# Scale and shift of a LayerNorm moved into the matmul that follows it, and factors formed from tiles already on the chip

## The chip, the cores and the metric

One program runs on one core of a Trainium2 chip. The core has five engines with their own in-order queues: TensorE (PE: matmuls, transposes; its weight loads, PEld, overlap them), VectorE (DVE), ScalarE (ACT), GpSimd (POOL) and SyncE (SP, which here only issues DMAs). They share an SBUF of 128 partitions; matmuls write to PSUM. The metric is the device time of one execution in microseconds (us), the median over the runs shown; lower is better.

## What is computed

One layer of a hybrid encoder on x of 512 tokens by 2048, in float32. Cut to what matters here:

```
h = rms_norm(x, g_mix)
q, k, v_sb, u, v_sg, gate_a, gate_b = split(h @ w_in)      # 1024 x5, 2048 x2 columns
o = stick_breaking_attention(rms(q) * g_q, rms(k) * g_k, v_sb)          # 8 heads
y_a = o @ w_oa
u, v = gelu(u), gelu(v_sg)
v = layer_norm(v, sgu_ln_g, sgu_ln_b)                      # over 1024 columns
w = where(mask, w_spatial, 0)                              # 8 groups of 128 x 128
mixed = einsum('gij,bcjgd->bcigd', w, chunks(v)) + b_spatial
y_b = (u * mixed) @ w_ob
x = x + (sigmoid(gate_a) * y_a + sigmoid(gate_b) * y_b) @ w_out
x = x + square(relu(rms_norm(x, g_ff) @ w_ff1)) @ w_ff2
```

The gain and the bias of the LayerNorm go by the column d of a group, the mixing sums over the token j. So gain[d] * (w @ v0) + bias[d] * (row sum of w) + b_spatial is the same number as w @ (v0 * gain + bias) + b_spatial, where v0 is v less its mean, times the reciprocal of its spread.

## The kernel before

**Split matmuls.** A float32 operand is held as two `float32r` tiles, hi and lo (`split_to`, L106: ACT casts hi at L108 or L111, DVE subtracts for lo at L109 or L112), and a product is three matmuls (`mm3`, L70: lines 72, 73, 74). Weights are loaded by SP, two 128-row pieces at a time (`weight`, L87: cast L94, subtraction L96).

**Stages.** `by_token` (L117) makes 512 columns of a projection for four blocks of 128 tokens in four PSUM accumulators (of five): eight weight loads, 24 matmuls each, then one evacuation per block. Its order is q, k, v of heads 0 to 3, then q, k, v of heads 4 to 7, then the two halves of `vg` (v_sg). Then come u and the gates, 256 columns at a time: the first pair with plain matmuls (`plain_pair`, L245), all others by a Strassen scheme (`strassen_columns`, L197) with seven products and three fork accumulators that `new_forks` opens (L288) in the second PSUM pool, `aux`, of three tiles. Then `ya`, `yb`, the output projection and the MLP.

**Work behind the matmuls.** `behind` is a queue of small steps; after each weight load's matmuls `step()` takes one, and `flush()` takes all that are left. Each engine gets its instructions about in the order in which they are written; a planner that knows dependences may let a ready one pass one that is not, but at run time every queue is in order.

- The attention of one half (`attention`, L521) is twelve such steps: `weights` (scores, sigmoids, a scan on DVE), `turn` (transposes, `aT` at L555) and `product` (L563), whose result `oT` POOL stores to DRAM (L569). That of half 0 runs beside the second q and k projections, that of half 1 beside `vg`.
- `save` (L481) adds hi and lo of the normalised input `hT` to a whole tile (L485) and stores it with POOL (L486) in `held_h`, four tiles to a step, in the first v projection.
- `gate_factors` (L596) fetches two of these whole tiles back with POOL (L478) and forms the four sums m7, m6, m4, m5 that the Strassen scheme needs for that pair (`factor`, L236: one DVE sum or difference at L242, then hi and lo). Eight such calls stand at steps 6, 8, 10, 11, 12, 13, 14 and 15 of the 16 steps of `vg`.
- `moved` (L587) copies some `hT` tiles out of the buffers for raw weights.

**The LayerNorm.** `evac_v` (L616) applies Gelu on ACT (L618) and leaves the eight tiles in SBUF. In the u stage `centred` (L633) takes their moments (`bn_stats` L636, `bn_aggr` L638) and normalises in place (L644); `normed` (L647) lets POOL multiply by the gain (L649), add the bias (L650), both held as broadcast rows, and store the tile (L651) in `held_v`. `spatial` (L665) transposes the mixing matrices (L668), masks them (L671 to L674) and splits them into `wsp`; it is a step of the u pair too.

**The mixing.** In the `ya` stage POOL fetches v and u again (`fetch_mix`), `split_mix` (L731) splits v, and `mixed` (L735) multiplies by the mixing matrices (L744, L746), adds the two PSUM halves and `bs`, the broadcast b_spatial, on DVE (L748, L750), and multiplies by u on POOL (L751). The evacuation of `ya` is a DVE product with the gate (L777).

**Buffers.** All tiles of 512 columns come from one pool, `slots`, of 64; twelve more are in `long`, where the first six `hT` pairs live. Raw weights have six buffers, of which three hold `hT` tiles 6 to 8 for a time.

Of the kernel before, what the change touches and what calls it, by code (L numbers as in the profile page):

```python
# [10 lines left out]
F32 = mybir.dt.float32  # L11
# [5 lines left out]
P = 128  # L17
# [5 lines left out]
SBW = 1024  # L23
# [12 lines left out]
def tile_hybrid_layer(ctx: ExitStack, tc: tile.TileContext, x, g_mix, w_in, g_q, g_k, ln_g, ln_b,  # L36
# [17 lines left out]
    def slot(name, dt=F32, pool=slots):  # L54
        return pool.tile([P, 512], dt, name=name, tag="slot")
# [10 lines left out]
    def f32(ap):  # L66
        return ap.bitcast(F32)
# [289 lines left out]


    gm = const.tile([16, P], F32, name="gm")
    gains = const.tile([32, P], F32, name="gains")  # L360
    gT = const.tile([P, 16], F32, name="gT")
    gT2 = const.tile([P, 32], F32, name="gT2")

    def turn_gains(src, dst):
        n = src.shape[0]
# [101 lines left out]
    win = w_in[0]  # L467


    held_h = dram.tile([KT, P, W], F32, name="held_h")  # L470
    held_o = dram.tile([HEADS, 2, P, W], F32, name="held_o")
    held_v = dram.tile([2, NTB, P, W], F32, name="held_v")
    held_g = dram.tile([(SGW + 2 * D) // P, P, W], F32, name="held_g")
# [4 lines left out]
        nc.gpsimd.dma_start(out=f32(t) if dt is F32R else t, in_=src)  # L478
        return t

    def save(k):  # L481
        t = slot("whole")
        for half, part in enumerate(hT[k]):
            hi, lo = (f32(x) for x in sides(part))
            nc.vector.tensor_tensor(out=t[:, half * HS:(half + 1) * HS], in0=hi, in1=lo, op=ALU.add)  # L485
        nc.gpsimd.dma_start(out=held_h[k], in_=t)  # L486

    def heads_of(c0, g0, half, name):

# [81 lines left out]
        steps = [[(weights, 0)], [], [(weights, 1)], [(turn, 0)], [(weights, 2)], [(product, 0), (turn, 1)], [(weights, 3)], [(product, 1), (turn, 2)], [], [(product, 2), (turn, 3)], [], [(product, 3)]]  # L571
        return [lambda fs=fs: [f(h) for f, h in fs] for fs in steps]

    for half in range(2):
        qT = heads_of(0, 16, half, "q")
        kT = heads_of(SBW, 24, half, "k")
        if half == 0:
            behind.extend([lambda k=k: [save(k + i) for i in range(4)] for k in range(0, KT, 4)])
        v = []
        by_token(win, 2 * SBW + half * W, hT_at, KT,  # L580
                 lambda tb, o, v=v: v.append(split(o, "v", rstd[:, tb:tb + 1])), "v")
        if half == 0:
            behind.extend(attention(half, qT, kT, v))

    hy = {}

    def moved(k):  # L587
        for half, part in enumerate(hT[k]):
            name = "y" + "12"[k % 2] + "12"[half]
            if LONG // 2 <= k < LONG // 2 + RAWH and name != "y12":  # L590
                t = slot("hT", F32R)
                nc.sync.dma_start(out=f32(t), in_=f32(part))
                part = t
            hy[name, k // 2] = part

    def gate_factors(k):  # L596
        whole = [fetched(held_h[2 * k + i], "whole") for i in range(2)]
        for name in ("m7", "m6", "m4", "m5"):
            factor(hy, whole, k, name, -1.0 if name in ("m7", "m4") else None)

    def at_steps(steps):
        behind.extend([lambda fs=steps.get(i, []): [f() for f in fs] for i in range(max(steps) + 1)])

    steps = collections.defaultdict(list)
    for i, f in enumerate(attention(half, qT, kT, v)):
        steps[i].append(f)
    for k in range(KT):
        steps[2 + k // 4].append(lambda k=k: moved(k))
    for k, i in enumerate((6, 8, 10, 11, 12, 13, 14, 15)):
        steps[i].append(lambda k=k: gate_factors(k))  # L610
    at_steps(steps)

    vg = {}
    VS = 3 * SBW + SGW
    for half in range(2):
        def evac_v(tb, o):  # L616
            t = slot("vg")
            nc.scalar.activation(out=t, in_=o, func=AF.Gelu, scale=rstd[:, tb:tb + 1])  # L618
            vg[tb, half] = t

        by_token(win, VS + half * W, hT_at, KT, evac_v, "vg")
    ref = state["load"]

    lng, lnb = [], []
    with tc.issue_after(ref.ins):
        for half in range(2):
            for src, dst, nm in ((ln_g, lng, "lng"), (ln_b, lnb, "lnb")):
                t = slot(nm)
                nc.sync.dma_start(out=t, in_=src[:, half * W:(half + 1) * W].to_broadcast([P, W]))
                dst.append(t)  # L630
    vn = {}

    def centred(tb):  # L633
        st = tiny(12, "st")
        for half in range(2):
            nc.vector.bn_stats(out=st[:, half * 6:half * 6 + 6], in_=vg[tb, half])  # L636
        mv = tiny(2, "mv")
        nc.vector.bn_aggr(out=mv, in_=st)  # L638
        ve = tiny(1, "ve")
        nc.vector.tensor_scalar(out=ve, in0=mv[:, 1:2], scalar1=EPS, scalar2=None, op0=ALU.add)  # L640
        r = rsqrt(ve, 1, "r")
        for half in range(2):
            t = vg[tb, half]
            nc.vector.tensor_scalar(out=t, in0=t, scalar1=mv[:, 0:1], scalar2=r, op0=ALU.subtract,  # L644
                                    op1=ALU.mult)

    def normed(tb, half):  # L647
        t = vg[tb, half]
        nc.gpsimd.tensor_tensor(out=t, in0=t, in1=lng[half], op=ALU.mult)  # L649
        nc.gpsimd.tensor_tensor(out=t, in0=t, in1=lnb[half], op=ALU.add)  # L650
        nc.gpsimd.dma_start(out=held_v[half, tb], in_=t)  # L651

    wsT = []
    with tc.issue_after(ref.ins):
        ws, bs = [], []
        for half in range(2):
            t = slot("ws")
            nc.sync.dma_start(out=t.rearrange("p (g j) -> p g j", g=4),
                              in_=w_sp[0, half * 4:half * 4 + 4].rearrange("g i j -> i g j"))
            ws.append(t)  # L660
            t = slot("bs")
            nc.sync.dma_start(out=t, in_=b_sp.rearrange("o g i -> o (g i)")[:, half * W:(half + 1) * W]
                              .to_broadcast([P, W]))
            bs.append(t)
    def spatial(half):  # L665
        t = aux("wsT")
        for g in range(4):
            nc.tensor.transpose(out=t[:, g * P:(g + 1) * P], in_=ws[half][:, g * P:(g + 1) * P],  # L668
                                identity=ident)
        m = slot("wsm")  # L670
        nc.vector.tensor_copy(out=m[:64, :], in_=t[:64, :])  # L671
        m3 = m.rearrange("p (g i) -> p g i", g=4)
        nc.vector.memset(m3[64:, :, :64], 0.0)
        nc.vector.tensor_copy(out=m3[64:, :, 64:],  # L674
                              in_=t.rearrange("p (g i) -> p g i", g=4)[64:, :, 64:])

        for i in range(2):
            pair = slot("wsp", F32R)
            p3 = pair.rearrange("p (g h i) -> p g h i", g=2, h=2)
            split_to(p3[:, :, 0, :], p3[:, :, 1, :], m3[:, 2 * i:2 * i + 2, :])  # L680
            wsT.append(pair)

    def gated(n, act, func, signs, inside):
        for c, (t, sign) in enumerate(zip(act, signs)):
# [15 lines left out]
    for c0, n, func in order:  # L700
        if forks is None:
            gated(n, plain_pair(win, c0, hy, "u"), func, (1.0, 1.0), False)
            flush()
            forks = new_forks(hy["y11", 0])
            for tb in range(NTB):
                for half in range(2):
# [23 lines left out]

    def split_mix(half):  # L731
        for tb in range(NTB):
            vn[tb, half] = split(vn[tb, half], "vn")

    def mixed(g):  # L735
        half, c = g // 4, (g % 4) * P
# [2 lines left out]
        for pair in range(2):  # L739

            o = aux("mix").rearrange("p (b h i) -> p b h i", b=2, h=2)
            for b in range(2):
# [2 lines left out]
                                 stop=False)  # L745
                nc.tensor.matmul(o[:, b, 1], lhsT=vl, rhs=both[:, :P], start=False, stop=True)  # L746
            t3 = t[:, pair * 2 * P:(pair + 1) * 2 * P].rearrange("p (b i) -> p b i", b=2)
            nc.vector.tensor_tensor(out=t3, in0=o[:, :, 1, :], in1=bs[half][:, c:c + P].unsqueeze(1)  # L748
                                    .to_broadcast([P, 2, P]), op=ALU.add)
# [301 lines left out]
```

## Time and profile before

| | us |
|---|---|
| median of 3 runs (2466.0 to 2468.88) | 2468.77 |
| the profiled execution | 2469.41 |
| its span, first to last instruction | 2467.7 |
| q, k, v and the attention of half 0 | about 0 to 307 |
| the two `vg` halves | 307 to 424 |
| the first u pair | 424 to 458 |
| Strassen pairs of u and the gates | 458 to 846 |
| `ya` | 845 to 945 |

The mean granted TensorE clock is 0.994 of full speed. The page gives the busy time of each engine and the chain of work that ended last; the view of waits tells for each engine which instruction stood idle, what it waited for, and how long in total; the timeline lists instructions in order of time, with the idle time before one and its releaser in brackets; the view by stretches gives the busy time of each engine in a window. Matmuls overlap in the pipeline, so a row's duration is longer than the distance to the next start.

### The profile page before, as it was taken

Reading aid. Unit: us, or ns where it says so; the run is one execution under the profiler, and the core shown is the slowest. Engines: PE = TensorE matmul, PEld = TensorE weight load, DVE = VectorE, ACT = ScalarE, POOL = GpSimd, SP = SyncE. Lnnn points to the kernel's source line nnn. Section 1 sums busy time; section 2 is a strip of 40 time slices with the busy share of each in tenths; the row PEclk is TensorE's granted clock in tenths of the full one; section 3 lists DMA queues with packets and bytes.
Section 4 is the critical chain, followed back from the end, with each engine's and each line's share of the span. In section 5 each row is a group of like instructions: output and inputs, shape, how many; then the busy total and the mean of one; then the engine's idle time right before and its main releaser. Section 6 shows DMA issues by size and latency. Waiting matters only on the chain.

```text
span 2467.7 us, 34420 instructions
## 1 busy us (share of the span) xinstructions
PE 2422.0 (98%) x12696; PEld 2082.2 (84%) x12696; DVE 1857.9 (75%) x2416; ACT 1196.6 (48%) x1759; POOL 450.8 (18%) x583
## 2 busy tenths in 40 slices
PE   9999998699999999999999999999999999999999
PEld 7888887589888888888888899888888888888887
DVE  4566465977778654534689888888888998989887
ACT  5333334355555422323377677777765443333333
POOL 0223121500000322200001000001014434312210
PEclk9999999899999999999999999999999999999999
DMA  5343335566666854434369888888995999877863
GB/s 180 94 154 103 94 108 165 137 168 161 158 164 160 292 168 141 150 128 145 95 175 234 231 235 223 228 228 228 225 290 205 315 325 293 254 221 208 247 183 94
DMA packets 444841, 469.45 MB, mean 190 GB/s; under 512 B 19920, under 2 KB 328192, under 8 KB 444672
## 3 DMA queue, kind: packets, MB, share of 16 engines
q1 hardware_dynamic: 355984, 331.95, 42.1%
q0 software_dynamic: 88400, 134.77, 23.2%
q8 instruction: 100, 1.64, 0.3%
q10 hardware_dynamic: 288, 0.52, 0.1%
q14 instruction: 69, 0.57, 0.1%
HBM read 378.04 MB, written 88.08 MB: 189 GB/s over the span
## 4 chain that ended last, share of the span: by engine, by line
PE 94%; DVE 3%; issue 1%; DMA 1%; ACT 1%; POOL 0%; DVEq 0%; SPq 0%; ACTq 0%; POOLq 0%
PE q L215 11%; PE fork L215 11%; PE q L73 11%; PE q L72 11%; PE q L74 11%; PE fork L218 6%; PE q L218 6%; PE xo L72 2%; PE xo L73 2%; PE xo L74 2%; PE v L74 1%; PE v L72 1%; PE v L73 1%; PE yb L74 1%; PE yb L72 1%
## 5 line engine op out<-in xcount | busy, mean ns | idle before, releaser
L108 ACT CAST w_hi<-w_raw 128x1024 fp32r<-128x1024 f32 (+1 forms) x576 | 604.8, 1050 | 667.1 <-PE q L73 333.4
L109 DVE TENSOR_TENSOR w_lo<-w_raw,w_hi 128x1024 fp32r<-128x1024 f32 (+1 forms) x576 | 701.2, 1220 | 172.4 <-ACT w_hi L108 165.9
L73 PE MATMUL q<-w_lo,ys 128*128 128x512 f32 x896 | 349.4, 390 | 0.9 <-DVE w_lo L109 0.8
L74 PE MATMUL q<-w_hi,ys 128*128 128x512 f32 x896 | 348.7, 389 | 0.0
L96 DVE TENSOR_TENSOR w_lo<-w_raw,w_hi 128x1024 fp32r<-128x1024 f32 x135 | 168.8, 1250 | 222.7 <-ACT w_hi L94 218.8
L72 PE MATMUL q<-w_hi,ys 128*128 128x512 f32 x896 | 312.1, 389 | 0.9 <-ACT w_hi L108 0.9
L94 ACT CAST w_hi<-w_raw 128x1024 fp32r<-128x1024 f32 x135 | 141.8, 1051 | 343.3 <-issue 66.9
L215 PE MATMUL q<-ys,w_hi 128*128 128x512 f32 x1048 | 271.1, 396 | 2.5 <-ACT fork L222 2.5
L183 POOL DMA_DIRECT2D w_raw<-in_w_ff_dram x58 | 80.9, 1395 | 908.0 <-DVE m L883 413.5
L215 PE MATMUL fork<-ys,w_hi 128*128 128x512 f32 x896 | 223.8, 392 | 0.0
L215 PEld LDWEIGHTS q<-ys,w_hi 128*128 128x128 f32 x1048 | 188.6, 191 | 34.7 <-ACT fork L222 2.7
L73 PEld LDWEIGHTS q<-w_lo,ys 128*128 128x128 f32 x896 | 168.2, 188 | 37.8 <-DVE w_lo L109 3.0
L72 PEld LDWEIGHTS q<-w_hi,ys 128*128 128x128 f32 x896 | 168.1, 188 | 36.2 <-ACT w_hi L108 1.3
L74 PEld LDWEIGHTS q<-w_hi,ys 128*128 128x128 f32 x896 | 168.2, 188 | 34.8
L215 PEld LDWEIGHTS fork<-ys,w_hi 128*128 128x128 f32 x896 | 163.6, 189 | 30.8
L951 POOL DMA_DIRECT2D ys<-store x224 | 127.0, 599 | 177.7 <-PE q L74 117.4
L218 PEld LDWEIGHTS q<-ys,w_lo 128*128 128x128 f32 x1048 | 143.3, 191 | 10.5
L218 PE MATMUL q<-ys,w_lo 128*128 128x256 f32 x1048 | 146.3, 282 | 0.0
L993 DVE SCALAR_TENSOR_TENSOR total<-q,plus,total 128x512 f32<-128x512 f32 x180 | 130.9, 743 | 0.4 <-PE q L74 0.4
L218 PEld LDWEIGHTS fork<-ys,w_lo 128*128 128x128 f32 x896 | 122.3, 190 | 8.7
L218 PE MATMUL fork<-ys,w_lo 128*128 128x256 f32 x896 | 125.3, 282 | 0.0
L181 DVE TENSOR_TENSOR w_raw<-w_raw 128x1024 f32<-128x1024 f32 x82 | 101.3, 1236 | 26.7 <-DMA w_raw<-in_w_ff_dram 10.3
(293 smaller groups left out, 4730.1 us busy)
## 6 DMA issues: line engine op xcount, KB each, us to landing
w_raw<-in_w_ff_dram SPq DMA_DIRECT2D x256, 512.0 KB, 5.7
w_raw<-in_w_in_dram SPq DMA_DIRECT2D x143, 512.0 KB, 3.9
ys<-store POOLq DMA_DIRECT2D x224, 256.0 KB, 6.8
w_raw<-in_w_ff_dram POOLq DMA_DIRECT2D x58, 512.0 KB, 6.9
store<-ys_hi SPq DMA_DIRECT2D x90, 256.0 KB, 4.5
store<-ys_lo SPq DMA_DIRECT2D x90, 256.0 KB, 5.5
w_raw<-in_w_out_dram SPq DMA_DIRECT2D x32, 512.0 KB, 3.6
store<-ys SPq DMA_DIRECT2D x44, 256.0 KB, 6.3
```

What stands on the lines that cost most here:

```text
L72: nc.tensor.matmul(o, lhsT=lh[0], rhs=rh[0], start=start, stop=False, **kw)
L73: nc.tensor.matmul(o, lhsT=lh[0], rhs=rh[1], start=False, stop=False, **kw)
L74: nc.tensor.matmul(o, lhsT=lh[1], rhs=rh[0], start=False, stop=stop, **kw)
L94: nc.scalar.copy(out=hi, in_=raw)
L96: nc.vector.tensor_tensor(out=lo, in0=raw, in1=f32(hi), op=ALU.subtract)
L108: nc.scalar.copy(out=hi, in_=src)
L109: state["lo"] = nc.vector.tensor_tensor(out=lo, in0=src, in1=f32(hi), op=ALU.subtract)
L181: nc.vector.tensor_tensor(out=self.a, in0=self.w11, in1=self.w21, op=ALU.add)
L215: nc.tensor.matmul(o, lhsT=hi[:, k, :], rhs=rhs[name][k], start=name == "y11" and k == 0, stop=False, skip_group_check=True)
L218: nc.tensor.matmul(o[:, :HS], lhsT=lo[:, k, :], rhs=rhs[name][k][:, :HS], start=False, stop=k == KH - 1, skip_group_check=True)
L951: nc.gpsimd.dma_start(out=f32(t), in_=store[f][HELD.index(name), p])
L993: nc.vector.scalar_tensor_tensor(out=a, in0=o, scalar=part, in1=a, op0=ALU.mult, op1=ALU.add)
```

## The change

The LayerNorm's gain and bias are no longer multiplied into v. They come in with the other gains (`gains` and `gT2` grow from 32 to 48 rows and columns). v is stored as it leaves the Gelu; its moments are kept, and `split_mix` centres and scales it with one DVE instruction before the split. `mixed` multiplies by the gain while it adds the halves, and the bias enters `bs` as bias times the row sums of the mixing matrix, which a matmul with ones makes. `spatial` and the loads it needs run in the first v projection. The whole tiles are no longer stored and fetched: `gate_factors` adds hi and lo of the resident `hT` itself, and three of its eight calls run in the second v projection.

```
-    gains = const.tile([32, P], F32, name="gains")
+    gains = const.tile([48, P], F32, name="gains")
...
+        nc.sync.dma_start(out=gains[32:40, :], in_=ln_g.rearrange("o (k p) -> (o k) p", p=P))
+        nc.sync.dma_start(out=gains[40:48, :], in_=ln_b.rearrange("o (k p) -> (o k) p", p=P))
...
-    def save(k):
+    def whole(k):
         t = slot("whole")
         for half, part in enumerate(hT[k]):
             hi, lo = (f32(x) for x in sides(part))
             nc.vector.tensor_tensor(out=t[:, half * HS:(half + 1) * HS], in0=hi, in1=lo, op=ALU.add)
-        nc.gpsimd.dma_start(out=held_h[k], in_=t)
+        return t
...
     def spatial(half):
...
+        rows = aux("rows")
+        nc.tensor.matmul(rows, lhsT=ones, rhs=m, start=True, stop=True)
+        for g in range(4):
+            c = slice(g * P, (g + 1) * P)
+            b = 40 + half * 4 + g
+            nc.vector.scalar_tensor_tensor(out=bs[half][:, c], in0=rows[:, c], scalar=gT2[:, b:b + 1],
+                                           in1=bs[half][:, c], op0=ALU.mult, op1=ALU.add)
...
     def gate_factors(k):
-        whole = [fetched(held_h[2 * k + i], "whole") for i in range(2)]
+        act = [whole(2 * k + i) for i in range(2)]
...
         if half == 0:
-            behind.extend([lambda k=k: [save(k + i) for i in range(4)] for k in range(0, KT, 4)])
+            behind.extend([load_spatial, lambda: None, lambda: spatial(0), lambda: spatial(1)])
+        else:
+            behind.extend([lambda k=k: gate_factors(k) for k in range(3)])
...
-    for k, i in enumerate((6, 8, 10, 11, 12, 13, 14, 15)):
+    for k, i in enumerate((8, 10, 12, 13, 14), 3):
         steps[i].append(lambda k=k: gate_factors(k))
...
             nc.scalar.activation(out=t, in_=o, func=AF.Gelu, scale=rstd[:, tb:tb + 1])
-            vg[tb, half] = t
+            nc.vector.bn_stats(out=stv[:, tb, half * 6:half * 6 + 6], in_=t)
+            nc.gpsimd.dma_start(out=held_v[half, tb], in_=t)
...
+    def moments():
+        for tb in range(NTB):
+            nc.vector.bn_aggr(out=mv[:, tb, :], in_=stv[:, tb, :])
+        ve = tiny(4, "ve")
+        nc.vector.tensor_scalar(out=ve, in0=mv[:, :, 1], scalar1=EPS, scalar2=None, op0=ALU.add)
+        nc.gpsimd.tensor_tensor(out=rv, in0=ve, in1=mhalf, op=ALU.pow)
...
-    behind.extend([lambda: [centred(tb) for tb in range(NTB)], lambda: None, lambda: spatial(0), lambda: spatial(1)])
+    behind.append(moments)
...
-            for tb in range(NTB):
-                for half in range(2):
-                    behind.extend([lambda tb=tb, half=half: normed(tb, half), lambda: None, lambda: None])
...
     def split_mix(half):
         for tb in range(NTB):
-            vn[tb, half] = split(vn[tb, half], "vn")
+            t = vn[tb, half]
+            nc.vector.tensor_scalar(out=t, in0=t, scalar1=mv[:, tb, 0:1], scalar2=rv[:, tb:tb + 1],
+                                    op0=ALU.subtract, op1=ALU.mult)
+            vn[tb, half] = split(t, "vn")
...
-            nc.vector.tensor_tensor(out=t3, in0=o[:, :, 1, :], in1=bs[half][:, c:c + P].unsqueeze(1)
-                                    .to_broadcast([P, 2, P]), op=ALU.add)
-            nc.vector.tensor_tensor(out=t3, in0=o[:, :, 0, :], in1=t3, op=ALU.add)
+            gain = gT2[:, 32 + g:33 + g]
+            nc.vector.scalar_tensor_tensor(out=t3, in0=o[:, :, 1, :], scalar=gain, in1=bs[half][:, c:c + P]
+                                           .unsqueeze(1).to_broadcast([P, 2, P]), op0=ALU.mult, op1=ALU.add)
+            nc.vector.scalar_tensor_tensor(out=t3, in0=o[:, :, 0, :], scalar=gain, in1=t3, op0=ALU.mult,
+                                           op1=ALU.add)
```

`centred`, `normed` and the broadcast loads of the gain and the bias are gone; `load_spatial` holds the four loads that stood behind `normed`.

More of the change, by code (lines that the diff above doesn't have):

```diff
@@ L359, in tile_hybrid_layer @@
     gm = const.tile([16, P], F32, name="gm")
-    gains = const.tile([32, P], F32, name="gains")
+    gains = const.tile([48, P], F32, name="gains")
     gT = const.tile([P, 16], F32, name="gT")
-    gT2 = const.tile([P, 32], F32, name="gT2")
+    gT2 = const.tile([P, 48], F32, name="gT2")
     def turn_gains(src, dst):
@@ L467, in tile_hybrid_layer @@
     win = w_in[0]
-    held_h = dram.tile([KT, P, W], F32, name="held_h")
     held_o = dram.tile([HEADS, 2, P, W], F32, name="held_o")
@@ L572, in attention @@
         return [lambda fs=fs: [f(h) for f, h in fs] for fs in steps]
-    for half in range(2):
-        qT = heads_of(0, 16, half, "q")
-        kT = heads_of(SBW, 24, half, "k")
-        if half == 0:
-            behind.extend([lambda k=k: [save(k + i) for i in range(4)] for k in range(0, KT, 4)])
[L579 to L596, printed above, removed]
-        whole = [fetched(held_h[2 * k + i], "whole") for i in range(2)]
-        for name in ("m7", "m6", "m4", "m5"):
-            factor(hy, whole, k, name, -1.0 if name in ("m7", "m4") else None)
@@ L601, in at_steps @@
[L601 to L608, printed above, removed]
-    for k, i in enumerate((6, 8, 10, 11, 12, 13, 14, 15)):
[L610 to L618, printed above, removed]
-            vg[tb, half] = t
[L621 to L655, printed above, removed]
+    wsT, ws, bs = [], [], []
+    def load_spatial():
         for half in range(2):
@@ L681, in spatial, with moved @@
             wsT.append(pair)
+        rows = aux("rows")
[5 more added lines that the diff above has]
+                                           in1=bs[half][:, c], op0=ALU.mult, op1=ALU.add)
+    hy = {}
+    def moved(k):
+        for half, part in enumerate(hT[k]):
+            name = "y" + "12"[k % 2] + "12"[half]
+            if LONG // 2 <= k < LONG // 2 + RAWH and name != "y12":
+                t = slot("hT", F32R)
+                nc.sync.dma_start(out=f32(t), in_=f32(part))
+                part = t
+            hy[name, k // 2] = part
@@ new lines, in gate_factors @@
+    def gate_factors(k):
+        act = [whole(2 * k + i) for i in range(2)]
+        for name in ("m7", "m6", "m4", "m5"):
+            factor(hy, act, k, name, -1.0 if name in ("m7", "m4") else None)
+    for half in range(2):
+        qT = heads_of(0, 16, half, "q")
+        kT = heads_of(SBW, 24, half, "k")
+        if half == 0:
+            behind.extend([load_spatial, lambda: None, lambda: spatial(0), lambda: spatial(1)])
+        else:
+            behind.extend([lambda k=k: gate_factors(k) for k in range(3)])
+        v = []
+        by_token(win, 2 * SBW + half * W, hT_at, KT,
+                 lambda tb, o, v=v: v.append(split(o, "v", rstd[:, tb:tb + 1])), "v")
+        if half == 0:
+            behind.extend(attention(half, qT, kT, v))
@@ new lines, in at_steps @@
+    def at_steps(steps):
+        behind.extend([lambda fs=steps.get(i, []): [f() for f in fs] for i in range(max(steps) + 1)])
+    steps = collections.defaultdict(list)
+    for i, f in enumerate(attention(half, qT, kT, v)):
+        steps[i].append(f)
+    for k in range(KT):
+        steps[2 + k // 4].append(lambda k=k: moved(k))
+    for k, i in enumerate((8, 10, 12, 13, 14), 3):
+        steps[i].append(lambda k=k: gate_factors(k))
+    at_steps(steps)
+    VS = 3 * SBW + SGW
+    stv = const.tile([P, NTB, 12], F32, name="stv")
@@ new lines, in tile_hybrid_layer, with evac_v @@
+    mv = const.tile([P, NTB, 2], F32, name="mv")
+    rv = const.tile([P, NTB], F32, name="rv")
+    for half in range(2):
+        def evac_v(tb, o):
+            t = slot("vg")
+            nc.scalar.activation(out=t, in_=o, func=AF.Gelu, scale=rstd[:, tb:tb + 1])
+            nc.vector.bn_stats(out=stv[:, tb, half * 6:half * 6 + 6], in_=t)
+            nc.gpsimd.dma_start(out=held_v[half, tb], in_=t)
+        by_token(win, VS + half * W, hT_at, KT, evac_v, "vg")
+    vn = {}
+    def moments():
[4 more added lines that the diff above has]
+        nc.gpsimd.tensor_tensor(out=rv, in0=ve, in1=mhalf, op=ALU.pow)
@@ L704, in tile_hybrid_layer @@
             forks = new_forks(hy["y11", 0])
-            for tb in range(NTB):
-                for half in range(2):
-                    behind.extend([lambda tb=tb, half=half: normed(tb, half), lambda: None, lambda: None])
         else:
```

## The prediction

> **What bounds the kernel now.** I read the page first, then TensorE's waits, then the timeline at each long wait.
>
> ```profile
> span 2467.7 us, 34420 instructions
> PE 2422.0 (98%) x12696; PEld 2082.2 (84%) x12696; DVE 1857.9 (75%) x2416; ACT 1196.6 (48%) x1759; POOL 450.8 (18%) x583
> PE 94%; DVE 3%; issue 1%; DMA 1%; ACT 1%; POOL 0%; DVEq 0%; SPq 0%; ACTq 0%; POOLq 0%
> ```
>
> The profiled execution took 2469.4 us, 1.7 more than its span and 0.6 more than the median of 2468.8. PE idles 2467.7 - 2422.0 = 45.7 us. Only three things can move the end: PE's idle time, its clock, and its matmuls. Where it idles (line waiting, releaser: total us, times, longest):
>
> ```profile
> PE fork L288 <- DVE wsm L674: 12.8, 2, 9.4
> PE u L72 <- ACT vg L618: 8.9, 1, 8.9
> PE aT L555 <- DVE oT_lo L109: 6.8, 1, 6.8
> PE ya L72 <- DVE merged_a L777: 1.8, 2, 1.5
> ```
>
> The first three, 28.5 us, all lie between 369 and 478 us, and each ends on work that the diff takes away or moves.
>
> ```profile
> 367.11 4.33 DMA whole<-held_h
> 371.52 0.88 DVE L242 TENSOR_TENSOR whole<-whole 128x256 f32<-128x256 f32 x2 [2.49 <-DMA whole<-held_h]
> 375.93 0.69 DVE L109 TENSOR_TENSOR oT_lo<-o,oT_hi 128x512 fp32r<-128x512 f32 x1
> 407.00 0.54 POOL L569 DMA_DIRECT2D held_o<-oT_hi  x1 [12.75 <-ACT oT_hi L108]
> 409.13 3.21 POOL L478 DMA_DIRECT2D whole<-held_h  x6
> 412.26 0.89 DVE L242 TENSOR_TENSOR whole<-whole 128x256 f32<-128x256 f32 x2 [2.57 <-DMA whole<-held_h]
> 423.50 0.39 PE L74 MATMUL vg<-w_hi,hT 128*128 128x512 f32 x1
> 423.73 0.28 PE L72 MATMUL u<-hT,w_hi 128*128 128x256 f32 x1
> 440.69 2.41 ACT L618 ACTIVATE vg<-vg,rstd 128x512 f32<-128x512 f32 x4
> 441.43 0.58 PE L72 MATMUL u<-hT,w_hi 128*128 128x256 f32 x1 [8.91 <-ACT vg L618]
> ```
>
> **Wait of 6.8.** DVE stands at its next instruction, gate factor 0, until the fetch of `whole` lands at 371.44; that factor's chain runs to 375.9, and only then does DVE reach `oT_lo`, which frees the PSUM tile that the transposes need. **Wait of 8.9.** Most fetches of `whole` are issued only after 407 us, because they queue on POOL behind stores of `oT`. So five factors run from 412 to 441 on DVE and ACT, and the Gelu evacuation of v, in ACT's queue behind them, starts at 440.69 although its matmuls ended at 423.7. The u product has 441.43 - 423.73 - 8.91 = 8.8 us of matmuls in hand before it needs that accumulator.
>
> ```profile
> 444.18 1.00 DVE L644 TENSOR_SCALAR vg<-vg,mv,r 128x512 f32<-128x512 f32 x2
> 449.23 2.94 DVE L644 TENSOR_SCALAR vg<-vg,mv,r 128x512 f32<-128x512 f32 x2
> 464.79 9.91 DVE L109 TENSOR_TENSOR wsp<-wsm,wsp 128x256 fp32r<-128x256 f32 x1 [0.53 <-ACT wsp L108]
> 475.76 0.41 DVE L109 TENSOR_TENSOR wsp<-wsm,wsp 128x256 fp32r<-128x256 f32 x1
> 471.24 3.17 POOL L650 TENSOR_TENSOR vg<-vg,lnb 128x512 f32<-128x512 f32 x2
> ```
>
> **Wait of 12.8.** The forks need PSUM tiles that the spatial transposes still hold until DVE copies them. DVE is late twice over: centring follows the late evacuation, and with POOL scaling and shifting beside it the same centring takes 1.47 us each instead of 0.50 (two to a row), and one split 9.91 instead of 0.41.
>
> After each wait the granted clock is half for some 4 us (stretch, length, busy by engine, then the clock, DMA share and GB/s):
>
> ```profile
> 376.00:382.00 6.00, 5.32 (x20) 4.32 (x21) 4.24 (x9) 5.01 (x9) 2.15 (x4) 0.60 0.53 178
> 441.00:446.00 5.00, 4.57 (x22) 4.57 (x23) 4.88 (x15) 2.11 (x4) 2.27 (x3) 0.53 0.34 107
> 477.00:482.00 5.00, 4.18 (x10) 3.35 (x11) 4.92 (x9) 2.28 (x4) 0.00 (x0) 0.50 0.24 83
> ```
>
> Lost work is (1 - clock) x length, less half of the idle time inside: 2.4 - 0.3, 2.35 - 0.2 and 2.5 - 0.4, so 6.3 us.
>
> **The change part by part.**
>
> ```profile
> L242 DVE TENSOR_TENSOR whole<-whole x32: 405/425/427, 371.5 to 439.6; 128x256 f32<-128x256 f32 x32
> L485 DVE TENSOR_TENSOR whole<-hT x26: 412/415/417, 132.9 to 144.5; 128x256 f32<-128x256 f32 x26
> L112 DVE SCALAR_TENSOR_TENSOR ys<-whole,ys x16: 416/425/427, 372.4 to 440.5; 128x256 fp32r<-128x256 f32 x16
> L109 DVE TENSOR_TENSOR ys<-whole,ys x16: 416/419/426, 373.8 to 440.9; 128x256 fp32r<-128x256 f32 x16
> L486 POOL DMA_DIRECT2D held_h<-whole x16: 539/539/782, 134.0 to 145.4; - x16
> L478 POOL DMA_DIRECT2D whole<-held_h x16: 536/537/586, 366.5 to 413.5; - x16
> 285.00:303.00 18.00, 18.00 (x83) 14.91 (x82) 4.38 (x5) 4.80 (x5) 0.00 (x0) 1.00 0.28 88
> 261.00:307.00 46.00, 46.00 (x214) 38.05 (x213) 21.21 (x28) 15.71 (x20) 7.96 (x8) 1.00 0.30 91
> 378.00:424.00 46.00, 46.00 (x211) 38.60 (x212) 25.78 (x47) 18.67 (x33) 9.04 (x17) 0.97 0.62 200
> 424.00:442.00 18.00, 13.00 (x30) 0.82 0.29 89
> ```
>
> *Gate factors.* The 32 sums (26 of one shape and 6 from `hT_both`) stay, 32 x 0.415 = 13.3 us of DVE, but move from the first v projection to each factor. The 16 stores and 16 fetches leave POOL, and with them the dependence on a landing. A factor costs DVE 4 x 0.415 + 4 x 0.425 + 2 x 0.425 + 2 x 0.419 = 5.05 us instead of 3.39. Three move into the second v projection: 15.1 us beside 21.2 already there of 46; between 285 and 303 (busy times in the order PE, weight load, DVE, ACT, POOL) DVE is busy 4.4 of 18, so about 1.5 us spill behind 303, beside the evacuation of v. Its cover is v's own matmuls and a fifth accumulator that the next projection may start on; without that it costs 1.5 us. Five remain from step 8: 25.3 us in place of seven factors' 23.7. DVE's 25.8 + 13.0 = 38.8 us of 378 to 442 (the last row has DVE alone) becomes 40.4 with 46 + 8.8 = 54.8 us to run in. So I take both waits as gone: 6.8 + 8.9. What is late next is the evacuation of v, with some 14 us to spare.
>
> *LayerNorm.* POOL's 16 multiplications and additions go, and eight centrings leave the u stage. `bn_stats` and the eight stores of v (0.54 us of POOL each, as L486's) move to the evacuation; no buffer waits on LayerNorm any more. The spatial transposes move to the first v projection: eight stay eight, their DVE work replaces the sums that left. SP gains two small loads of gains, issues four spatial loads earlier and loses four broadcasts; in that projection it issues one weight load per 24 matmuls, so the cover is 24 x 0.23 = 5.5 us (423.50 to 423.73 is one matmul). Uncovered, an issue costs 0.45 us, as the first row below shows.
>
> ```profile
> 441.51 0.45 SPq L662 DMA_DIRECT2D bs<-in_b_spatial_dram  x1
> L447 PE MATMUL rp<-dg,ones x8: 272/275/276, 71.8 to 72.6; 128*128 128x128 f32 x8
> L748 DVE TENSOR_TENSOR smix<-mix,bs 128x256 f32<-128x256 f32 x16 | 6.5, 420 | 7.3 <-PE mix L746 7.1
> 842.00:936.00 94.00, 50.13 (x80) 1.00 0.60 212
> ```
>
> With nothing ahead of the forks any more, I take the 12.8 as gone, and all three half-clock stretches: 6.3.
>
> *New on PE.* Two row-sum matmuls of 512 float32 columns, a form that the trace lacks. Below: one ordinary 512-column matmul, 0.23 each. Above: eight 128-column float32 matmuls start within 0.8 us, so four make 0.4. I take 0.4 each, the same element type: 0.8 us. Their eight row corrections on DVE (at most 0.425 each, 3.4 us, half the width of the row named) find the room that the sums left.
>
> *New in the ya stage.* Eight tensor_scalars, 0.5 us each as at 444.18, before the splits; the 32 mixing instructions become scalar forms of 0.425 against 0.420, nothing. Each batch of four is 2.0 us ahead of `w_lo` and `merged_a` on DVE, for which PE already waits 1.8. DVE is busy 50.1 of 94 (last row above), so the cost is between nothing and 4.0, and the wait cannot shrink because nothing leaves that queue; I take 1.0, a quarter of the upper end, since DVE is free nearly half the time and each batch is only late if it meets a `merged_a`.
>
> **Sum:** -28.5 - 6.3 + 0.8 + 1.0 = -33.0. 2469.4 - 33.0 = **2436.4 us**; against the median it would be 2435.8, inside the rounding of these terms.
>
> **Rivals.**
>
> *DVE keeps the evacuation late.* Factors carry more DVE work, and if the last ones still stand in ACT's queue ahead of the Gelu, the 8.9 and its 2.1 of clock stay: 2447.4. For it: the casts and the Gelu share one in-order queue. Against: 14 us to spare.
>
> *The fetch was not the cause.* The factor chain itself (371.5 to 375.9, 4.4 us, longer by its sums) may stand ahead of `oT_lo` wherever it is put: 6.8 + 2.1 stay, 2445.3. Against: DVE waited 2.49 us for the landing in that gap alone, and factor 0 is no longer there.
>
> *POOL beside DVE in the mixing.* By 449.23 against 444.18, a tensor_scalar beside POOL's work costs 0.97 more; eight make 7.8 us, all of it on PE at worst: 2444.2. POOL multiplies and fetches there, but less densely than at 449.
>
> The Trainium skill, page "SBUF — State Buffer", section "Who interferes with whom", has a rule for this: a VectorE instruction in a two-port mode (tensor_scalar can be) or with two SBUF inputs contends with GpSimd, and whichever is issued first blocks the other for its whole length. The 9.91 us against 0.41 agrees with it; by the rule the change gives back in ya part of what it wins before the forks, and the time is 2444.2 rather than 2436.4.
>
> *Buffers run out (the slower side).* The pool `slots` has 64. By the code, at the third `weights` of the second attention half there live 14 hT, 4 moved, 8 q and k, 8 v, 3 beta and 6 aT, 43. The change adds 12 factor tiles, 4 `wsp` and 2 `bs`: 61, and that step wants 3 beta, a keep and a rest. If ACT stands at the first that has no buffer, weight casts queue behind it, and PE loses up to one step, 5.5 us, per attention step. One to four such steps give 2442 to 2458; five or six, 2464 to 2469, no change; from seven on (steps 2 to 8 of the twelve), 2436.4 + 38.5 = 2475 and slower. Against: beta, keep and rest recycle within a step, and the product that frees 6 comes one step later.
>
> **Chances.** Forecast 0.52 (2432 to 2442). Late evacuation 0.13, chain 0.07, POOL 0.08, one to four starved steps 0.05; five or six 0.08; seven or more 0.07. The first five make 0.85, the range: 2432 (no ya cost, a little regained at 899) to 2458 (four starved steps, or two rivals at once). A measurement of this kernel tells 0.2%, 4.9 us, from no change: faster 0.85, same 0.08, slower 0.07.
>
> **What would show it.** Right: PE's waits no longer list L288, u at L72 or L555, and the clock stays near 1.00 from 300 to 500 us; no POOL work between 441 and 476 but stores; the split of `wsp` near 0.41. Wrong: PE idle anywhere in the vg projection with ACT or SP waiting for a buffer; the Gelu still behind a cast; tensor_scalars of 1 us or more around 870 and 906 and a longer wait for `merged_a`.

## The result, and the profile after

The changed kernel takes 2434.81 us (median of 4 runs, 2434.08 to 2436.34) against 2467.44 for the kernel before in the same comparison: 32.6 us less, a ratio of 0.9869 with a 95% interval from 0.9851 to 0.9886. The forecast was 2436.4. The profiled execution took 2434.23 us. Among all executions two were slow, one of the kernel before (2668 us) and one of E11 (7293 us): medians count them, ratios don't.

Two lines of the page of after: the span, and the busy time of each engine.

```profile
span 2432.5 us, 34311 instructions
PE 2415.5 (99%) x12700; PEld 2077.2 (85%) x12700; DVE 1844.9 (76%) x2421; ACT 1198.0 (49%) x1759; POOL 414.9 (17%) x532
```

The span fell by 35.2 us. PE's idle time went from 45.7 to 2432.5 - 2415.5 = 17.0, so 28.7 of the 35.2 was waiting. PE's busy time fell by 6.5 although it has more records; the granted clock rose from 0.994 to 0.999, and the three stretches that stood near half clock before now stand at 1.00. What PE still waits for (line waiting, releaser: total, times, longest):

```profile
PE gp L367 <- DMA gm<-in_g_mix_dram: 6.0, 1, 6.0
PE q L215 <- ACT fork L222: 2.5, 1, 2.5
PE ya L72 <- DVE merged_a L771: 2.4, 2, 1.8
PE q L72 <- ACT w_hi L108: 0.9, 1, 0.9
```

The three long waits are all gone. The first line is the start of the program; of the others only the wait for `merged_a` has grown, from 1.8 to 2.4. The work that the long waits ended on now stands in the timelines of DVE and ACT like this:

```profile
371.48 0.68 DVE L109 TENSOR_TENSOR oT_lo<-o,oT_hi 128x512 fp32r<-128x512 f32 x1
373.81 1.43 DVE L486 TENSOR_TENSOR whole<-hT_both 128x256 f32<-128x256 f32 x4
421.38 0.39 ACT L108 CAST ys<-whole 128x256 fp32r<-128x256 f32 x1
421.68 2.42 ACT L661 ACTIVATE vg<-vg,rstd 128x512 f32<-128x512 f32 x4
```

`oT_lo` is made ahead of the first factor of this stage and not behind it. The Gelu starts at 421.68 instead of 440.69, but it still stands directly behind a factor's cast in ACT's queue, which the prediction had named as a sign of being wrong; that matters below. One stretch of the view by windows (busy in the order PE, weight load, DVE, ACT, POOL, then the clock):

```profile
424.00:442.00 18.00, 18.00 (x148) 17.83 (x147) 8.94 (x13) 4.83 (x6) 3.59 (x4) 1.00 0.72 182
```

PE is busy throughout at the full clock. In this stretch of time the clock was 0.82 before, and DVE had 13.0 us of work instead of 8.9. The groups of the mixing matrices and of the row sums, and the row sums in PE's timeline:

```profile
L109 DVE TENSOR_TENSOR wsp<-wsm,wsp x4: 419/423/426, 150.0 to 157.7; 128x256 fp32r<-128x256 f32 x4
L606 PE MATMUL rows<-wsm,ones x4: 592/592/592, 152.5 to 158.3; 128*128 128x512 f32 x4
```

```profile
152.26 0.40 PE L74 MATMUL v<-w_hi,hT 128*128 128x512 f32 x1
152.50 1.02 PE L606 MATMUL rows<-wsm,ones 128*128 128x512 f32 x2
153.36 0.60 PE L591 MATMUL wsT<-ident,ws 128*128 128x128 f32 x4
```

No split of `wsp` is stretched any more (the worst was 9.91 us). The two row-sum matmuls stand as four records, two to a matmul, and one takes PE 153.36 - 152.50 = 0.86 us.

### The profile page after: what moved, and what is told of

Its sections match the earlier page's. It is cut to its first block, busy times and chain, and to the rows that moved or that the text cites. A ratio compares the mean times of both kernels' runs of the same rounds, so it can differ in the third digit from the quotient of the medians.

```text
span 2432.5 us, 34311 instructions
## 1 busy us (share of the span) xinstructions
PE 2415.5 (99%) x12700; PEld 2077.2 (85%) x12700; DVE 1844.9 (76%) x2421; ACT 1198.0 (49%) x1759; POOL 414.9 (17%) x532
## 4 chain that ended last, share of the span: by engine, by line
PE 83%; DVE 1%; ACT 0%; issue 0%; POOL 0%; DVEq 0%; POOLq 0%; ACTq 0%
PE q L215 11%; PE fork L215 11%; PE q L72 10%; PE q L73 10%; PE q L74 10%; PE fork L218 6%; PE q L218 6%; PE xo L74 2%; PE xo L72 2%; PE xo L73 2%; PE yb L74 1%; PE yb L73 1%; PE yb L72 1%; PE ya L72 1%; PE ya L73 1%; PE ya L74 1%
## 5 line engine op out<-in xcount | busy, mean ns | idle before, releaser
L72 PE MATMUL q<-w_hi,ys 128*128 128x512 f32 x896 | 312.0, 389 | 0.9 <-ACT w_hi L108 0.9
L72 PEld LDWEIGHTS q<-w_hi,ys 128*128 128x128 f32 x896 | 168.1, 188 | 36.1 <-ACT w_hi L108 1.3
L73 PEld LDWEIGHTS q<-w_lo,ys 128*128 128x128 f32 x896 | 168.2, 188 | 35.2 <-DVE w_lo L109 0.4
L218 PE MATMUL q<-ys,w_lo 128*128 128x256 f32 x1048 | 145.7, 282 | 0.0
L74 PE MATMUL q<-ys,w_lo 128*128 128x256 f32 x400 | 113.2, 283 | 0.0
```

Source lines behind the costliest of these rows:

```text
L72: nc.tensor.matmul(o, lhsT=lh[0], rhs=rh[0], start=start, stop=False, **kw)
L73: nc.tensor.matmul(o, lhsT=lh[0], rhs=rh[1], start=False, stop=False, **kw)
L74: nc.tensor.matmul(o, lhsT=lh[1], rhs=rh[0], start=False, stop=stop, **kw)
L218: nc.tensor.matmul(o[:, :HS], lhsT=lo[:, k, :], rhs=rhs[name][k][:, :HS], start=False, stop=k == KH - 1, skip_group_check=True)
```

## The experiments

Seven versions first, as a table: whether the factor steps, the LayerNorm and the source of the whole tiles are the old or the new ones. Medians in us; in the comparisons of the other rows the kernel before took 2467.16 to 2467.85, and the ratios further down are to those.

| factor steps | LayerNorm | whole tiles | kernel | us |
|---|---|---|---|---|
| old | old | fetched | before | 2467.44 |
| old | old | resident | E1 | 2463.89 |
| old | no gain, no bias | fetched | E2 | 2450.98 |
| old | new | resident | E4 | 2449.35 |
| new | old | fetched | E7 | 2442.36 |
| new | new | fetched | E3 | 2434.89 |
| new | new | resident | after | 2434.81 |

### E1 and E3: is the fetch the cause of the two early waits?

E1 is the kernel before with nothing changed but the source of the whole tiles: no sums in the first v projection, no store, no fetch. The eight factors keep their old steps.

```
-        nc.gpsimd.dma_start(out=held_h[k], in_=t)
+        return t
...
-        whole = [fetched(held_h[2 * k + i], "whole") for i in range(2)]
+        act = [whole(2 * k + i) for i in range(2)]
```

> The kernel before with one part of the change: factors from the resident hi and lo, at the old eight steps; LayerNorm and the spatial transposes as before. Theory (the fetch caused both early waits): PE's waits at L555 (6.8) and at u L72 (8.9) go, with 4.2 us of half clock; POOL still scales and shifts beside DVE, so the forks wait 9 to 13 us; 2467 - 20 = 2447, at most 2451. Rival (the factor chain itself stands ahead of oT_lo): 6 us or more stay at L555, 2454 to 2458. Rival (the casts stand ahead of the Gelu whatever feeds them): 8 us or more stay at u L72, 2456 to 2460.

It took 2463.89 us, ratio 0.9986 (0.9977 to 0.9995), 3.3 less than before. The time lies above the ranges of all three expectations: each rival left one of the two waits, and here both stay, each shorter than its rival had it. PE's waits, then DVE's and ACT's timelines, in E1:

```profile
PE fork L288 <- DVE wsm L671: 12.7, 2, 9.3
PE u L72 <- ACT vg L615: 6.0, 1, 6.0
PE aT L554 <- DVE oT_lo L109: 5.3, 1, 5.3
```

```profile
368.46 1.40 DVE L484 TENSOR_TENSOR whole<-hT 128x256 f32<-128x256 f32 x4
374.38 0.69 DVE L109 TENSOR_TENSOR oT_lo<-o,oT_hi 128x512 fp32r<-128x512 f32 x1
436.49 0.39 ACT L108 CAST ys<-whole 128x256 fp32r<-128x256 f32 x1
436.78 2.42 ACT L615 ACTIVATE vg<-vg,rstd 128x512 f32<-128x512 f32 x4
```

No landing is left to wait for, and both waits stay, 1.5 and 2.9 us shorter. The factor written at step 6 still holds DVE from 368.46 to 374.38, and `oT_lo` is next. The Gelu comes at 436.78, only 3.9 earlier than before. E3 is the reverse: the changed kernel, with the whole tiles stored and fetched again.

```
-        return t
+        nc.gpsimd.dma_start(out=held_h[k], in_=t)
...
-        act = [whole(2 * k + i) for i in range(2)]
+        act = [fetched(held_h[2 * k + i], "whole") for i in range(2)]
```

> The changed kernel with the whole tiles stored in the first v projection and fetched again by POOL for each factor, at the new steps. Theory (the fetch is the cause): the five fetches that stand beside the attention queue on POOL behind the stores of oT; one of the waits at L555 or the attention's PSUM tiles (about 7) and that at u (about 9) come back with their half clock, 2435 + 11 to 20 = 2446 to 2455. Rival (the new steps did it): no new PE wait over 2 us, 2435 to 2438.

2434.89 us, 0.9869 (0.9853 to 0.9886): the time of after. One wait in E3's list of PE is new:

```profile
PE vg L72 <- DVE v_lo L112: 1.8, 1, 1.8
```

That one is the spill of the three factors behind the second v projection: fetched, they end late enough to hold its evacuation, and E7 shows the same line. So the fetch lengthens the two early waits, by 1.5 and 2.9 us, but it doesn't make them: neither goes when it goes, and neither comes back with it.

### E4, E8, E9 and E11: the place of the factors

E4 is the changed kernel with all eight factors at their old steps, none in the second v projection.

```
-            behind.extend([lambda k=k: gate_factors(k) for k in range(3)])
...
-    for k, i in enumerate((8, 10, 12, 13, 14), 3):
+    for k, i in enumerate((6, 8, 10, 11, 12, 13, 14, 15)):
```

> The changed kernel with the eight factors at the steps of before (6, 8, 10 to 15, none in the second v projection). New theory (the factors' place, not their source, makes the two early waits): PE waits 5 us at the attention's transposes and 6 us at u again, with some 4 us of half clock, as the kernel with resident factors at the old steps did: 2435 + 15 = 2450. Rival (the LayerNorm's part removed them): no wait over 2 us there, 2433 to 2438.

2449.35 us, 0.9922 (0.9905 to 0.9938). PE's waits in E4:

```profile
PE u L72 <- ACT vg L659: 5.3, 1, 5.3
PE aT L556 <- DVE oT_lo L109: 5.2, 1, 5.2
```

Both are back, almost as long as in E1, in a kernel without a fetch. E8 moves one factor only, from step 8 to step 6:

```
-    for k, i in enumerate((8, 10, 12, 13, 14), 3):
+    for k, i in enumerate((6, 10, 12, 13, 14), 3):
```

> The changed kernel with the first of the five factors of the vg projection at step 6 instead of 8. Theory (a factor written ahead of the attention's third product stands ahead of oT_lo on DVE): PE waits about 5 us at the transposes, with 2 us of half clock, and not at u: 2435 + 7 = 2442. Rival (only the number of factors in the projection counts): no wait over 2 us, 2433 to 2438.

2441.04 us, 0.9892 (0.9876 to 0.9908). A line of PE's waits, and two of DVE's timeline, in E8:

```profile
PE aT L556 <- DVE oT_lo L109: 5.2, 1, 5.2
```

```profile
371.48 0.88 DVE L242 TENSOR_TENSOR whole<-whole 128x256 f32<-128x256 f32 x2
375.93 0.69 DVE L109 TENSOR_TENSOR oT_lo<-o,oT_hi 128x512 fp32r<-128x512 f32 x1
```

The whole wait for `oT_lo` is this one step. The product at issue is the second of the four, not the third as the expectation says: it stands in step 7, and `oT_lo` at 375.93 is the second of four. At step 6 the factor is written ahead of it, so DVE has it first, and `oT_lo` comes at 375.93 instead of 371.48. The wait of u does not come back with it. But a factor ahead of an `oT_lo` need not cost anything. In after the third and the fourth `oT_lo` (383.09 and 398.63) stand directly behind one; the fourth in DVE's timeline:

```profile
398.19 0.42 DVE L109 TENSOR_TENSOR ys<-whole,ys 128x256 fp32r<-128x256 f32 x1
398.63 0.69 DVE L109 TENSOR_TENSOR oT_lo<-o,oT_hi 128x512 fp32r<-128x512 f32 x1
```

PE waits for neither: behind the third it has matmuls of `vg` to run until its next transposes at 388.15. So the order on DVE cost time only at the one `oT_lo` whose tile PE needed at once.

The wait of u was asked in E9 (later steps) and E11 (two factors in v, six in `vg`):

```
E9   -    for k, i in enumerate((8, 10, 12, 13, 14), 3):
     +    for k, i in enumerate((8, 10, 12, 14, 15), 3):
E11  -            behind.extend([lambda k=k: gate_factors(k) for k in range(3)])
     +            behind.extend([lambda k=k: gate_factors(k) for k in range(2)])
...
     -    for k, i in enumerate((8, 10, 12, 13, 14), 3):
     +    for k, i in enumerate((8, 10, 11, 12, 13, 14), 2):
```

> The changed kernel with the last two factors one step later, at 14 and 15 instead of 13 and 14. In the changed kernel the Gelu of v starts 3.8 us after its matmuls end, 5 us before u needs the accumulator. If the casts of the last factor hold it in ACT's queue, it starts later by up to one factor, about 4 us: PE waits 0 to 2 us at u, 2434 to 2438. If the margin were as large as predicted (14 us), nothing would change, and the Gelu would stay within 4 us of the end.

> The changed kernel with two factors in the second v projection instead of three, and six in vg at 8 and 10 to 14. Theory (DVE works the factors off without a break, so the Gelu waits for the count, not for the steps): it starts one factor, 4 to 5 us, later, some 8 us after its matmuls, and PE waits 0 to 2 us at u: 2434 to 2438. Rival (the steps pace the factors): the Gelu starts within 4 us of its matmuls' end, as in the changed kernel.

E9 took 2433.87 us, 0.9863 (0.9849 to 0.9878), E11 2434.36, 0.9863 (0.9842 to 0.9884). The Gelu's group in after (its last instruction starts at 423.4) and in E9, then ACT's timeline and a line of PE's waits in E11:

```profile
L661 ACT ACTIVATE vg<-vg,rstd x8: 680/690/701, 374.8 to 423.4; 128x512 f32<-128x512 f32 x8
```

```profile
L661 ACT ACTIVATE vg<-vg,rstd x8: 677/688/700, 374.2 to 422.8; 128x512 f32<-128x512 f32 x8
```

```profile
426.51 0.39 ACT L108 CAST ys<-whole 128x256 fp32r<-128x256 f32 x1
426.81 2.41 ACT L661 ACTIVATE vg<-vg,rstd 128x512 f32<-128x512 f32 x4
```

```profile
PE u L72 <- ACT vg L661: 0.3, 1, 0.3
```

In E9 later steps change nothing: DVE works the factors from step 10 on off one behind the other, whatever step they are written at. That is what its expectation allowed for a large margin, but it says nothing of the margin. E11 does: one factor more in this stage puts the Gelu back by 426.81 - 421.68 = 5.1 us, one factor's length, and PE begins to wait. The number that counts is that of the factors written at step 10 or later. Counted from the start of the last `vg` matmul in PE's timeline to the Gelu in ACT's:

| factors at step 10 or later | whole tiles | kernel | Gelu, us after the last matmul | wait of u |
|---|---|---|---|---|
| 6 | fetched | before | 17.2 | 8.9 |
| 6 | resident | E1, E4 | 14.3 | 6.0, 5.3 |
| 5 | resident | E11 | 9.2 | 0.3 |
| 4 | fetched | E3 | 7.1 | none |
| 4 | resident | after, E8, E9 | 4.0 | none |

Each factor more puts the Gelu back by 5.1 us, and the fetch by 3, at the old steps as at the new. At the new steps those 3 us are covered: the change has just under 5 us to spare.

### E2, E5 and E7: the wait of the forks

E2 is the kernel before without POOL's multiplication and addition; it leaves the LayerNorm's gain and bias out.

```
-        nc.gpsimd.tensor_tensor(out=t, in0=t, in1=lng[half], op=ALU.mult)
-        nc.gpsimd.tensor_tensor(out=t, in0=t, in1=lnb[half], op=ALU.add)
```

> The kernel before with POOL's sixteen multiplications by the gain and additions of the bias left out, all else as it was. Theory (POOL beside DVE makes the fork wait): centring takes 0.5 us each, the split of wsp 0.41 instead of 9.91, and the forks wait under 4 us instead of 12.8; 2467 - 9 to 11 = 2456 to 2458; the waits of 6.8 and 8.9 stay. Rival (the late evacuation alone makes it): the forks still wait 9 us or more, 2464 to 2468.

2450.98 us, 0.9934 (0.9919 to 0.9949): 16.2 less than before, where the theory expected 9 to 11. PE's waits, then DVE's groups for the centring and the split, in E2:

```profile
PE u L72 <- ACT vg L618: 8.9, 1, 8.9
PE aT L555 <- DVE oT_lo L109: 7.1, 1, 7.1
```

```profile
L644 DVE TENSOR_SCALAR vg<-vg,mv,r x8: 529/548/640, 444.2 to 450.7; 128x512 f32<-128x512 f32 x8
L109 DVE TENSOR_TENSOR wsp<-wsm,wsp x4: 416/418/426, 456.4 to 462.2; 128x256 fp32r<-128x256 f32 x4
```

The list has no line for L288 any more, though the evacuation is as late as before (u still waits 8.9). The three numbers of a group are the shortest, the median and the longest in ns: the centring takes 0.55 us and the split 0.42. The expectation was too small because it left up to 4 us of the wait and counted no clock: all of the 12.8 went, and with it the half clock behind it (1.00 from 446 to 500 us). E4's list, with the new LayerNorm and a late evacuation, has no line for L288 either. E5 moves the spatial loads, transposes and row sums of the changed kernel back beside the u pair.

```
-            behind.extend([load_spatial, lambda: None, lambda: spatial(0), lambda: spatial(1)])
+            pass
...
+    with tc.issue_after(state["load"].ins):
+        load_spatial()
...
-    behind.append(moments)
+    behind.extend([moments, lambda: None, lambda: spatial(0), lambda: spatial(1)])
```

> The changed kernel with the four spatial loads, the transposes, the masks and the row sums back in the u pair. Theory (the fork wait came from POOL beside DVE alone): the forks wait under 2 us and the time is 2433 to 2438. Rival (the transposes that hold the PSUM tiles make it): the forks wait 5 us or more, 2441 to 2448.

2435.77 us, 0.9869 (0.9854 to 0.9884). The split in E5, at its old place:

```profile
L109 DVE TENSOR_TENSOR wsp<-wsm,wsp x4: 417/418/426, 435.6 to 443.8; 128x256 fp32r<-128x256 f32 x4
```

It is as fast there, and PE has no wait at L288. E7 is the kernel before with the new factor steps alone, so with an early evacuation and POOL's arithmetic.

```
+        else:
+            behind.extend([lambda k=k: gate_factors(k) for k in range(3)])
...
-    for k, i in enumerate((6, 8, 10, 11, 12, 13, 14, 15)):
+    for k, i in enumerate((8, 10, 12, 13, 14), 3):
```

> The kernel before with the new steps for its fetched factors (three in the second v projection, five at 8, 10, 12, 13 and 14), LayerNorm as before. Theory (the place): the waits at the attention's transposes and at u go, 8.9 + 6.8 + 4 of half clock; POOL is still beside DVE, but the centring starts some 15 us earlier against u, so the forks wait 3 to 13 us: 2467 - 19 to 31 = 2436 to 2448. Rival (a late LayerNorm keeps all three): 2460 or more.

2442.36 us, 0.9897 (0.9883 to 0.9912). Its wait of the forks, and its centring and split:

```profile
PE fork L288 <- DVE wsm L676: 7.4, 2, 6.6
```

```profile
L646 DVE TENSOR_SCALAR vg<-vg,mv,r x8: 533/993/1519, 426.1 to 447.6; 128x512 f32<-128x512 f32 x8
L109 DVE TENSOR_TENSOR wsp<-wsm,wsp x4: 415/958/1516, 451.5 to 461.6; 128x256 fp32r<-128x256 f32 x4
```

The two early waits are gone, the forks' is shorter but stays, and centring and split take 0.99 and 0.96 us in the median. So the early evacuation alone leaves 7.4 of the 12.8; taking POOL's arithmetic away leaves nothing; where `spatial` stands makes no difference once that arithmetic is gone. Moving `spatial` with POOL's arithmetic left in was not run.

### E6: buffers

```
-SLOTS = 64
+SLOTS = 62
```

> The changed kernel with 62 buffers in slots instead of 64. If the attention's tiles already wait for buffers, two fewer cost at least one step of 5.5 us of PE idle in the vg projection, 2440 or more, with ACT or SP waiting there for a buffer. If they don't, the time stays within 0.2%, 2430 to 2440, and PE has no new wait over 2 us.

2439.7 us, 0.9886 (0.9872 to 0.9901). The `vg` stage and the end of the program in the view by windows, in E6 and in after:

```profile
307.00:424.00 117.00, 115.65 (x576) 97.80 (x575) 85.93 (x161) 52.44 (x104) 19.25 (x29) 1.00 0.39 121
1600.00:2438.70 838.70, 829.19 (x4022) 699.77 (x4020) 735.29 (x848) 403.85 (x496) 196.55 (x291) 1.00 0.79 237
```

```profile
307.00:424.00 117.00, 116.80 (x586) 98.87 (x585) 87.82 (x165) 53.64 (x105) 20.50 (x31) 1.00 0.38 123
1600.00:2432.50 832.50, 826.90 (x4018) 699.16 (x4016) 733.88 (x845) 404.40 (x496) 206.19 (x291) 1.00 0.78 238
```

With 64 buffers PE idles 0.2 us in the whole `vg` stage, so no missing buffer holds it there. With 62 it idles 1.2 more there and 9.5 instead of 5.6 from 1600 us to the end, most of which is the MLP. So the second branch came, at its very edge: no step of 5.5 us is lost in `vg`, and no single new wait is over 2 us, but the program is 4.9 us longer than after. A larger pool was not run.

### E10: the place of the mixing steps

The mixing steps are spread so that none stands just ahead of a `ya` evacuation.

```
-        steps[5 + g + g // 4].append(lambda g=g: mixed(g))
+        steps[(5, 6, 8, 9, 10, 12, 13, 14)[g]].append(lambda g=g: mixed(g))
```

> The changed kernel with the eight mixing steps of ya at 5, 6, 8, 9, 10, 12, 13, 14 instead of 5 to 8 and 10 to 13, so that none stands at the last step of a column block, ahead of that block's evacuation on DVE. Theory (the wait of 2.4 us for merged_a is the mixing's DVE work ahead of the evacuation): the wait falls under 0.6 us, 2431 to 2434. Rival (the new centring on DVE makes it): the wait stays at 2 us or more, 2434 to 2436.

2431.33 us (2431.15 to 2431.41), 0.9852 (0.9836 to 0.9867): the lowest median of all. Its interval overlaps that of after, but all four runs lie below all of after's. DVE's timeline in after, then in E10:

```profile
862.58 0.87 DVE L741 SCALAR_TENSOR_TENSOR smix<-mix,gT,bs 128x256 f32<-128x256 f32 x2
863.36 0.87 DVE L743 SCALAR_TENSOR_TENSOR smix<-mix,gT,smix 128x256 f32<-128x256 f32 x2
866.89 2.48 DVE L771 TENSOR_TENSOR merged_a<-ya,gate 128x512 f32<-128x512 f32 x4
```

```profile
862.04 0.69 DVE L109 TENSOR_TENSOR sT_lo<-smix,sT_hi 128x512 fp32r<-128x512 f32 x1
862.64 2.48 DVE L771 TENSOR_TENSOR merged_a<-ya,gate 128x512 f32<-128x512 f32 x4
```

`merged_a` comes 4.3 us earlier, and the list of PE's waits in E10 has no line for `ya`. So the wait came from the mixing's instructions ahead of `merged_a`, and not from the new centring, which E10 still has. The kernel before has its mixing at the same steps and a wait of 1.8 there; it was not run with the new ones. A row of it, next to the one at 863.36 above:

```profile
896.66 0.74 DVE L750 TENSOR_TENSOR smix<-mix,smix 128x256 f32<-128x256 f32 x2
```

Two of the old mixing instructions took 0.74 us, two of the new 0.87. Four of the new stand between a weight's subtraction and `merged_a`, 0.25 us longer together, and that is what the longer of the two waits grew by (1.5 to 1.8).

## Why the prediction came out, and where its reasons failed

**The sum.** Predicted -33.0, measured -35.2 in the span and -32.6 between the medians; the profiled execution of before took longer than any of the four runs in the comparison, that of after was near the shortest. The three waits, 28.5, went in full, as predicted. The clock gave more than the 6.3: PE's busy time fell 6.5 with 1.7 of row sums added, so about 8.2, an estimate from busy times whose ends are modelled. That the sum came so near is in part luck: the clock was 1.9 short one way, the row sums 0.9 the other.

**The signs.** Those of being right came: L288, L555 and u at L72 are off PE's list, the clock is 1.00 from 300 to 500, POOL only issues two transfers from 441 to 476, and the splits take 0.42. But of the signs of being wrong one came too, the Gelu behind a cast, and another in part: one tensor_scalar of eight takes 1.46 us, and the wait for `merged_a` grew. Neither cost what was feared, for the reasons below.

**The two early waits: size right, cause wrong.** The step that failed is "The 16 stores and 16 fetches leave POOL, and with them the dependence on a landing ... So I take both waits as gone". E1 takes the fetch away and keeps 5.3 and 6.0 of the 6.8 and 8.9; E3 and E7 keep the fetch and have neither wait. What took them away is the step that the prediction costed as a move of DVE work: three factors into the second v projection, and none left at step 6. Both stood in the same diff, so the 15.7 came out by luck and not by the reason given. E8 shows the first wait to be that one factor ahead of `oT_lo`; E4 and E11 show the second to be how many factors from step 10 on ACT has ahead of the Gelu. The 2.49 us that DVE waited for the landing was real, but behind it stood the factor's own chain, 4.4 us before and 5.9 in E1, that had to run in any case; E1 gains 3.3 us in all, and on top of the other parts the resident tiles gain nothing that can be measured (after against E3): they take away a wait of 1.8 behind the second v projection and bring the Gelu 3 us forward, where it was covered already.

The rival "the fetch was not the cause" had this mechanism. It expected the wait to stay because the chain would stand ahead of `oT_lo` "wherever it is put", and that half was wrong: the change puts it behind. Its 2445.3 did not come. What the prediction held against it in passing, that "factor 0 is no longer there", was the true reason for the first wait to go.

**"Some 14 us to spare".** This counted DVE's room over the whole stretch, as if factors could end late in it. The Gelu is bound by its place in ACT's queue, behind the last cast, and E11 puts the margin at just under 5 us. The rival "DVE keeps the evacuation late" was nearer than its 0.13 said: one factor more starts it.

**The 12.8 before the forks: right, though one of its two reasons would have done.** "DVE is late twice over" holds: E7 takes 5.4 off with the earlier evacuation alone. But the second reason is enough by itself: E2 removes POOL's arithmetic, leaves the evacuation late, and the wait is gone. The move of `spatial`, for which the prediction said that nothing stands ahead of the forks any more, gains nothing once POOL's arithmetic is gone (E5).

The Trainium skill, page "SBUF — State Buffer", section "Who interferes with whom", says that a VectorE instruction with two SBUF inputs contends with a GpSimd instruction that reads SBUF. E2 and E5 agree: 0.42 us for the split with POOL's arithmetic gone, 9.91 beside it. The size goes beyond a block of one instruction's length, which is how the prediction used the rule: POOL's additions beside the split take 3.17 us for two, so a split of 9.91 us ran beside several of them. The rival that `ya` pays it back did not come. The new centring in after:

```profile
L723 DVE TENSOR_SCALAR vn<-vn,mv,rv x8: 539/541/1460, 827.4 to 858.2; 128x512 f32<-128x512 f32 x8
```

One of eight is stretched, in the pair at 857.67, beside one of POOL's multiplications by u (857.84 to 859.36). Beside the six ahead of that pair POOL has no such multiplication.

**The small terms.** The row sums were put at 0.8 and cost 2 x 0.86 = 1.7: the eight records of `rp` from which 0.4 came are four matmuls, each recorded twice, so the bound was half of what it should have been. The `ya` stage was put at 1.0 and cost 2.4 - 1.8 = 0.6. The 1.0 was for the new centring, which E10 clears; the "nothing" for the mixing's scalar forms, priced at 0.425 us each from a row with both inputs in SBUF, was a term: with one input in PSUM they take 0.48 (L741 and L743). The spill of 1.5 us of the three factors behind the second v projection, costed at nothing, did not show in after: PE's list has no wait there. The slower side, buffers running out, did not come; E6 says that two buffers fewer cost 4.9 us, more of it towards the end of the program than in the attention steps where the prediction looked.

## What to carry to other kernels

When an engine waits for a transfer just before a stall, ask what stands behind the transfer in that engine's queue: if a chain of the same length runs there anyway, removing the transfer gains little (here 1.5 us of 6.8), and moving the chain past the urgent instruction gains the whole wait. Helper work belongs behind the instruction that frees an accumulator which TensorE needs next; ahead of one that it needed later it cost nothing here. The last evacuation that shares a queue with it limits how much of it a stage can take. Elementwise work on GpSimd was paid for here by VectorE beside it, so folding it into 32 instructions that run anyway, at 0.06 us more for each, took away a wait of 12.8 us.

## What the runs showed of the hardware

A float32 matmul of 512 columns (not split) holds PE for 0.86 us where an ordinary one of this kernel starts every 0.23, and it leaves two records: 12700 matmuls in after against 12696 for two that were added. One DVE instruction beside POOL's elementwise work can be stretched far beyond twice its length: a split of 0.42 us took 9.91 in the kernel before, though at most 1.5 in E7. And on 256 columns DVE's form with a scalar and a tensor (L743) takes 0.48 us where the plain sum of two tensors (L750) took 0.41, one of the inputs being in PSUM both times.
